# Two weight tiles of the first up chunk split into memory outside the ring

## The chip, the cores and the metric

The kernel runs on one core of a Trainium2 chip. The metric is the device time of one execution in microseconds (us). Times are the median of several executions; one further execution is recorded by the hardware profiler, and all rows quoted below are of that one.

## The reference

One decoder layer on 256 positions with width 2048, in float32:

```
h = rmsnorm(x);  p = h @ w_in                      # 2048 x 4160
A = 8 heads of dilated sliding-window attention from p
B = 8 heads of latent attention from p (w_uq, w_ukv)
x = x + rmsnorm(concat(A, B) @ w_out) * g1         # 2048 x 2048
h = rmsnorm(x)
x = x + rmsnorm(square(relu(h @ w_up)) @ w_down) * g2   # 2048 x 8192, 8192 x 2048
```

The change lies at the seam between `@ w_out` with its norm and the first columns of `@ w_up`.

## The kernel before, in words

**Products.** Each float32 matrix is split into a coarse part (`hi`) and a remainder (`lo`), and a product is three matmuls: hi·hi, lo·hi and hi·lo. One matmul takes 128 rows of the inner dimension and 512 columns. The 256 positions are two blocks, b = 0 and b = 1, of 128.

**Weights.** The class `Weights` holds a list of all weight tiles in the order of their use. Each tile is loaded by an SP DMA (SyncE's queue) into one of 5 `raw` buffers, and `split` or `split_gain` makes its two parts: ACT writes `hi` (L314, or L318 where a gain is multiplied in), DVE writes `lo` (L315 or L319). `hi` and `lo` come from a ring of 8 buffers each (`W_BUFS`), given out in turn. The order of the work on each engine is the order in which the program writes its instructions (the schedule is manual): what `emit` writes earlier stands earlier in ACT's, DVE's and SP's queues.

`get(i)` calls `emit(i + 1 + ahead)`, which writes the load and the split of every tile up to that index that isn't written yet, but at most 8 tiles beyond the first one that PE still needs (`limit`). `free(i)` tells that the last matmul of tile i has been written. `ahead` is 6; from the end of the out projection's block 0 until the end of the residual of block 1 it is 4 (`AHEAD_NORM`).

**The seam.** The out projection goes by chunks of 512 columns with 8 weight tiles each, of two 128-row blocks (I call the last chunk's tiles out 0 to out 7). In the last chunk out 0 to 2 are used for both blocks in turn, and then out 3 to 7 for block 0 and again for block 1, so that block 0's result is complete 5 tiles earlier (`APART[0]`). The up product's first chunk is 1024 columns in 16 tiles of 128 rows (up 0 to up 15), each worth 6 matmuls a block. Here up 0 to 6 are used for block 0, then up 0 to 6 for block 1, and then the rest for both in turn (`APART[1]` = 7). Thus up 0 to 6 stay in the ring until block 1's pass over them.

**The residual.** When block b of the last out chunk is complete, `out_evac` squares it on ACT (`junko`) and multiplies it by the gain on DVE (`yg`, L898). The generator `residual(b)` then makes the norm: DVE sums (`ssr`, L937) and scales (`t_post`, L505), POOL takes the power (`rstd_post`, L506), DVE updates the first two quarters of x (`x`, L943), and after that for each quarter n = 0 to 3: PE transposes it (`ht`, L308), DVE updates quarter n + 2 (n = 0 and 1 only), ACT writes `hT_hi` (L314), DVE writes `hT_lo` (L315). Quarter n holds the inner rows of up tiles 4n to 4n + 3. Behind the quarters follow four squares on ACT (`junkx`, L963), a sum (`ssr`, L965) and a scale (`t_pre`, L505) for the next norm. Residual 0 starts at the end of block 0's last matmul, residual 1 four planned microseconds after block 1's. `Flow` places these steps between matmuls by a clock that only matmuls and transposes advance (`pump` after every three matmuls); a weight split costs nothing on it.

The change uses two pieces of memory. `mixT` (a hi and a lo tile, 16 blocks of 256 columns) holds the heads' results, which the out projection reads; blocks 0 to 3 are read by out 0 and out 1. `po` is a pool of the out projection (gains, yg, x). Both pools are released just before up 8 is used, and a pool `up` takes their place.

Of the kernel before, what the change touches and what calls it, by code (L numbers as in the profile page):

```python
# [19 lines left out]
F32R = mybir.dt.float32r  # L20
# [6 lines left out]
P = 128  # L27
# [18 lines left out]
CW = 1024  # L46
# [30 lines left out]
APART = (5, 7)  # L77

FINE = 6

X_PIECES = ((2, 1, 1), (3, 2, 2), (5, 4, 3), (8, 7, 3), (11, 10, 3), (14, 13, 3))

# [53 lines left out]
class Flow:  # L136
# [3 lines left out]
    def __init__(self):  # L140
        self.clock = 0.0
        self.chains = []
# [34 lines left out]
class Weights:  # L177


    def __init__(self, nc, pool, split, bufs, ahead):  # L180
        self.nc, self.pool, self.split_fn = nc, pool, split
        self.bufs, self.limit, self.ahead = bufs, bufs, ahead
        self.specs, self.tiles, self.done = [], [], []
        self.first, self.after = {}, {}

    def plan(self, *spec):

# [11 lines left out]
        return raw  # L199

    def emit(self, upto):
        upto = min(upto, self.done.index(False) + self.limit, len(self.specs))
        while len(self.tiles) < upto:
            i = len(self.tiles)
            spec = self.specs[i]
            make = len(spec) == 1
            for f in self.first.pop(i, ()):
                f()
            if not make:
                src, nk, n, g = (*spec, None)[:4]  # L210
                w = nk * n
                raw = self.load(src if len(src.shape) == 3 else src.rearrange("(k p) n -> p k n", p=P), w, f"raw{i}")
                for f in self.after.pop(i, ()):
                    f()
            hi = self.pool.tile([P, CW], F32R, tag="hi", bufs=self.bufs, name=f"hi{i}")
            lo = self.pool.tile([P, CW], F32R, tag="lo", bufs=self.bufs, name=f"lo{i}")
            if make:
                spec[0](hi, lo)
                self.tiles.append((hi, lo))
                continue  # L220

            def v(t):
                return t[:, :w].rearrange("p (k n) -> p k n", k=nk)

            cuts = [(o, min(o + 512, w)) for o in range(0, w, 512)] if i < FINE else [(0, w)]
            for o, e in cuts:
                self.split_fn(hi[:, o:e], lo[:, o:e], raw[:, o:e], g)
            self.tiles.append((v(hi), v(lo)))
# [43 lines left out]
def layer(nc, tc, io):  # L272
    flow = Flow()

    def pool(name, side, **kw):
        return tc.alloc_tile_pool(name=name, bufs=1, side=side, **kw)
# [48 lines left out]
    weights = Weights(nc, wp, split, W_BUFS, W_AHEAD)  # L325
# [20 lines left out]
    def up_weight(j, k):  # L346
        return io["w_up"][k * P:(k + 1) * P, j * CW:(j + 1) * CW]

    late = {}
# [32 lines left out]
    def seven_up(j, kp):  # L382
        def load():
            if UP_PAIRS[j][kp] == "raw":
                return [weights.load(up_weight(j, 2 * kp + i), CW, f"raw_w{j}_{kp}{i}") for i in range(2)]
            return load_two(late[UP_PAIRS[j][kp]], nc.gpsimd if (j, kp) > (1, 0) else nc.sync,
                            io["w_up"][2 * kp * P:(2 * kp + 2) * P, j * CW:(j + 1) * CW])

        return seven(load, lambda: [late["up"].tile([P, CW], F32, tag="T", bufs=2, name=f"{n}{j}_{kp}") for n in "tu"])
# [21 lines left out]
    def plan_seven(fetch_sums, fs, after, more=(), late_sums=0, last=()):  # L411

        at = max(len(weights.specs) - SUMS_AHEAD, after)
        fetch, sums = fetch_sums
        for n, f in (*more, (0, fetch), (-late_sums, sums), *((0, f) for f in last)):
            weights.first.setdefault(at - n, []).append(f)
        return [weights.plan(f) for f in fs], len(weights.specs)
# [3 lines left out]
    wide_u, after = [], 0  # L421
    for j in range(FF // CW):
        wide_u.append([])
        for what, k in UP_STEPS[j]:
            if what == "k":

                ts = [weights.plan(up_weight(j, k), 1, CW, *([gcol[:, 8 + k:9 + k]] if j < 2 or k >= 2 * max(N_SEVEN) else []))]
            else:
                ts, after = plan_seven(*seven_up(j, k), after, (), SUMS_AHEAD + 1 if not k and N_SEVEN[j - 1] else 0)
            wide_u[j].append((what, k, ts))  # L430

    def down_weight(c, k):
        return io["w_down"][k * P:(k + 1) * P, c * CW:(c + 1) * CW]

    def seven_down(c, kp):
        def load():

            n = DOWN_SEVEN[c].index(kp)
            raw = dpl["ab"]
            if n % 2:  # L440
                raw = late["u01" if c else "c"]
            return load_two(raw, nc.gpsimd if c or n > 1 else nc.sync, io["w_down"][2 * kp * P:(2 * kp + 2) * P, c * CW:(c + 1) * CW])

        return seven(load, lambda: [late["st"][:, i * CW:(i + 1) * CW] for i in range(2)])

    dpl, left, skeep, wide_d = {}, {}, {}, []
    for c in range(2):
        wide_d.append([])
        for what, k in DOWN_STEPS[c]:
            if what == "k":  # L450
                ts = [weights.plan(down_weight(c, k), 1, CW)]
            else:
                q, parts_q, back = [lambda c=c, k=k, f=f: f(c, k) for f in (down_sums, down_split, down_back)]
                more = {"last": (back,)} if c and k in SHARED else {"more": ((2, q), (1, parts_q))}
                ts, after = plan_seven(*seven_down(c, k), after, **more)
# [8 lines left out]
    def proj(aT, chs, name, order=None, need=None, bank_of=None):  # L464
# [6 lines left out]
        for c, t, b in order:  # L471
# [4 lines left out]
            if need:  # L476
                need(k0 + kp - 1, b)
            if i[0] < FINE:
                hl = [(0, 0), (1, 0)], [(0, 1)]
# [33 lines left out]
    mixT = [mix.tile([P, HA + HB, S], F32R, name=f"mixT_{w}") for w in ("hi", "lo")]  # L513
# [201 lines left out]
    for half in range(2):  # L715
        qkv = {}
        for nms in (("qk", "v") if not half else "qkv"):
            accs = [acc for _, _, acc in proj(xT, [ch_a[half, nms]], f"{nms}{half}",
                                              bank_of=at_bank if (half, nms) == (0, "v") else None)]
            for i, nm in enumerate(nms):  # L720
                if half and nm == "v":
                    flow.finish(*heads)
                if not half and nm != "v":
                    t = early.tile([P, NB + 1, 512], F32, name=f"{nm}_{half}")
                else:
                    t = pa.tile([P, NB + (nm != "v"), 512], F32, tag=nm, name=f"{nm}_{half}")
# [134 lines left out]
    for what, ch in ch_b:  # L861
        if what == "qr":
            flow.finish(q_chain)
        if what in ("qr", "v0", "v1"):
            if what == "qr":
                qr = lat.tile([P, NB, HB, RB], F32, tag="cq", name="qr")
            for _, b, acc in proj(latT["q" if what == "qr" else "kv"], [ch], what):
                if what == "qr":
                    out = qr[:, b].rearrange("p h d -> p (h d)")
                else:  # L870
                    i = 4 * int(what[1])
# [4 lines left out]
        else:  # L876
            t, i = qT if what[0] == "q" else kT, 4 * int(what[1])
# [96 lines left out]
    def h_done(k, b):  # L974
        flow.until(lambda: 4 * parts[b] > k)

    res = [None] * NB
    for ns in ((0, 1), (2,), (3,)):
        if len(ns) == 2:
# [3 lines left out]
        for c, b, acc in proj(mixT, [ch_o[n] for n in ns], f"o{ns[0]}", order, heads_done):  # L983
            n = ns[c]
            if not late:
# [5 lines left out]
                po = late["po"] = pool("po", "right")  # L991
# [198 lines left out]
    for j in range(FF // CW):  # L1190
# [9 lines left out]
        for t, b in order:  # L1200
            what, k, tiles = steps[t]
# [189 lines left out]
    for g in (GT - 2, GT - 1):  # L1391
        for b, n in PARTS:
            for kk in range(4):
                k = 4 * g + kk
# [48 lines left out]
def build(nc, arrays):  # L1443
    io = {n: nc.dram_tensor(f"in_{n}", a.shape, mybir.dt.from_np(a.dtype), kind="ExternalInput").ap()
          for n, a in arrays.items()}
    io["out"] = nc.dram_tensor("out_0", (S, D), F32, kind="ExternalOutput").ap()
    with tile.TileContext(nc) as tc, tc.manual_schedule():
        layer(nc, tc, io)
# [12 lines left out]
```

## Time and profile before

| | |
|---|---|
| median of 3 runs | 1023.99 us (1022.15 to 1024.4) |
| profiled execution, its own time | 1021.68 us |
| its span | 1019.9 us |
| granted TensorE clock | 0.998 |
| PE (matmul) busy | 1009.6 us, 99% of the span |
| DVE busy | 839.7 us, 82% |
| ACT busy | 625.3 us, 61% |
| POOL busy | 98.3 us, 10% |
| DMA | 261 GB/s mean |

The rows of a timeline give start, duration, engine, line, operation, the tiles out<-in, shapes, the count, and in brackets how long the engine sat idle before it and what released it. A matmul's duration reaches over the next one's start, because matmuls are pipelined; the distance of starts tells how fast PE goes. Likewise on DVE and ACT one instruction's end overlaps the next one's start a little, so costs in a queue are taken as distances of starts.

### The profile page before, as it was taken

What the parts mean: (1) busy time and instruction counts of PE and PEld (TensorE: products, weight loads), DVE (VectorE), ACT (ScalarE), POOL (GpSimd) and SP (SyncE); (2) the same over time, 40 slices, a digit from 0 to 9 for tenths busy, and PEclk for the clock granted to TensorE, in tenths of its full rate; (3) what the DMA queues carried; (4) which work ended last, traced back from release to release, by engine and by line L of the source; (5) the groups of instructions that cost most, each with busy time, mean ns of one, the idle gap of its engine ahead of it and who ended that gap; (6) DMA issues with size and microseconds to landing.
All of it is one profiled execution on the core that took longest, in us unless ns stands there. A gap on an engine that the chain in (4) does not pass through costs nothing.

```text
span 1019.9 us, 13300 instructions
## 1 busy us (share of the span) xinstructions
PE 1009.6 (99%) x4678; PEld 842.4 (83%) x4678; DVE 839.7 (82%) x1125; ACT 625.3 (61%) x822; POOL 98.3 (10%) x156
## 2 busy tenths in 40 slices
PE   9999999999999999999999999999999999999996
PEld 6888889898888788888888888888888888888885
DVE  6676747676656779998999989898999989999885
ACT  6575436555454568576766776676666665767661
POOL 0020202002101200000010100000110000211100
PEclk9999999999999999999999999999999999999999
DMA  8977759555687477777988979679989867888952
GB/s 296 368 250 263 247 164 310 181 166 187 206 309 212 173 295 242 260 259 243 295 270 276 286 223 297 195 254 353 341 272 390 292 237 247 310 299 327 370 188 82
DMA packets 108850, 266.02 MB, mean 261 GB/s; under 512 B 9456, under 2 KB 28400, under 8 KB 108144
## 3 DMA queue, kind: packets, MB, share of 16 engines
q1 hardware_dynamic: 65584, 175.14, 50.1%
q0 software_dynamic: 19824, 70.27, 20.8%
q10 hardware_dynamic: 23376, 19.78, 6.2%
q8 instruction: 36, 0.59, 0.2%
q14 instruction: 30, 0.25, 0.1%
HBM read 232.12 MB, written 33.03 MB: 260 GB/s over the span
## 4 chain that ended last, share of the span: by engine, by line
PE 96%; DVE 1%; issue 1%; DMA 1%; ACT 0%; SPq 0%; POOL 0%; DVEq 0%; POOLq 0%; ACTq 0%
PE acc_u L304 26%; PE y L304 25%; PE acc_o L304 8%; PE md L304 6%; PE m L304 6%; PE acc_v L304 5%; PE acc_qk L304 4%; PE acc_q L304 3%; PE acc_k L304 3%; PE acc_ckv L304 3%; PE acc_cq L304 2%; PE sc_b L304 1%; PE acc_qr L304 1%; PE y L1329 1%; DMA raw<-in_w_in 1%
## 5 line engine op out<-in xcount | busy, mean ns | idle before, releaser
L315 DVE TENSOR_TENSOR lo<-raw,hi 128x1024 fp32r<-128x1024 f32 (+2 forms) x205 | 233.6, 1158 | 68.6 <-ACT hi L314 67.2
L314 ACT ACTIVATE hi<-raw 128x1024 fp32r<-128x1024 f32 (+2 forms) x205 | 202.8, 1004 | 76.1 <-DMA raw<-in_w_in 19.1
L304 PE MATMUL acc_u<-hi,hT_lo 128*128 128x512 f32 x386 | 150.3, 389 | 0.5 <-DVE hT_lo L315 0.5
L304 PE MATMUL acc_u<-hi,hT_hi 128*128 128x512 f32 x386 | 150.7, 390 | 0.0
L304 PE MATMUL acc_u<-lo,hT_hi 128*128 128x512 f32 x386 | 150.2, 389 | 0.0
L304 PE MATMUL y<-hi,uhi 128*128 128x512 f32 x358 | 139.3, 389 | 0.0
L304 PE MATMUL y<-lo,uhi 128*128 128x512 f32 x358 | 139.3, 389 | 0.0
L304 PE MATMUL y<-hi,ulo 128*128 128x512 f32 x358 | 139.3, 389 | 0.0
L318 ACT ACTIVATE hi<-raw,gcol 128x1024 fp32r<-128x1024 f32 x86 | 96.8, 1148 | 32.2 <-DMA raw<-in_w_up 12.0
L319 DVE SCALAR_TENSOR_TENSOR lo<-raw,gcol,hi 128x1024 fp32r<-128x1024 f32 x86 | 106.6, 1274 | 9.8 <-ACT hi L318 9.7
L304 PEld LDWEIGHTS acc_u<-hi,hT_lo 128*128 128x128 f32 x386 | 72.4, 188 | 15.9 <-DVE hT_lo L315 0.9
L304 PEld LDWEIGHTS acc_u<-hi,hT_hi 128*128 128x128 f32 x386 | 72.5, 188 | 14.9
L304 PEld LDWEIGHTS acc_u<-lo,hT_hi 128*128 128x128 f32 x386 | 72.5, 188 | 14.8
L304 PEld LDWEIGHTS y<-hi,ulo 128*128 128x128 f32 x358 | 67.2, 188 | 14.0
L304 PEld LDWEIGHTS y<-lo,uhi 128*128 128x128 f32 x358 | 67.2, 188 | 14.0
L304 PEld LDWEIGHTS y<-hi,uhi 128*128 128x128 f32 x358 | 67.2, 188 | 13.8
L315 DVE TENSOR_TENSOR lo<-st_down,hi 128x1024 fp32r<-128x1024 f32 x46 | 55.0, 1220 | 1.1 <-ACT hi L314 1.1
L304 PE MATMUL acc_o<-hi,mixT_hi 128*128 128x512 f32 x128 | 51.3, 401 | 0.0
L314 ACT ACTIVATE hi<-u 128x1024 fp32r<-128x1024 f32 (+1 forms) x33 | 32.3, 979 | 30.1 <-PE acc_u L304 12.3
L304 PE MATMUL md<-hi,s 128*128 128x512 f32 x138 | 50.0, 389 | 0.0
L304 PE MATMUL acc_o<-hi,mixT_lo 128*128 128x512 f32 x128 | 49.9, 390 | 0.0
L304 PE MATMUL acc_o<-lo,mixT_hi 128*128 128x512 f32 x128 | 49.8, 389 | 0.0
(353 smaller groups left out, 2042.3 us busy)
## 6 DMA issues: line engine op xcount, KB each, us to landing
raw<-in_w_up SPq DMA_DIRECT2D x86, 512.0 KB, 4.9
raw<-in_w_down SPq DMA_DIRECT2D x82, 512.0 KB, 6.1
raw<-in_w_in SPq DMA_DIRECT2D x55, 512.0 KB, 5.6
ab<-in_w_up POOLq DMA_DIRECT2D x17, 1024.0 KB, 7.2
raw<-in_w_out SPq DMA_DIRECT2D x32, 512.0 KB, 4.8
ab_down<-in_w_down POOLq DMA_DIRECT2D x11, 1024.0 KB, 9.3
ulo<-ukeep POOLq DMA_DIRECT2D x20, 512.0 KB, 6.0
rkeep<-r ACTq DMA_DIRECT2D x28, 256.0 KB, 3.7
```

The source lines that it names most:

```text
L304: nc.tensor.matmul(out, a, b, start=start, stop=stop)
L314: nc.scalar.activation(hi, src, AF.Copy)
L315: nc.vector.tensor_tensor(out=lo, in0=src, in1=hi.bitcast(F32), op=OP.subtract)
L318: nc.scalar.activation(hi, src, AF.Copy, scale=g)
L319: nc.vector.scalar_tensor_tensor(out=lo, in0=src, scalar=g, in1=hi.bitcast(F32), op0=OP.mult, op1=OP.subtract)
L1329: nc.tensor.matmul(out, a[x], w[z], start=False, stop=(x, z) == (1, 0), skip_group_check=True)
```

## The change

Tiles up 3 and up 4 no longer take buffers of the ring. `hi` and `lo` of up 3 are blocks 0 to 3 of the two `mixT` tiles; those of up 4 are two new tiles in the pool `po`. In `emit`, a lent tile doesn't count towards the limit of 8, and it is written whether the ring is full or not. Nothing is added to or taken from what is computed, loaded or split.

```
+LENT = 3, 4
...
     def emit(self, upto):
-        upto = min(upto, self.done.index(False) + self.limit, len(self.specs))
+        upto = min(upto, len(self.specs))
         while len(self.tiles) < upto:
             i = len(self.tiles)
+            own = [j for j in range(self.done.index(False), i) if j not in self.lent]
+            if i not in self.lent and len(own) >= self.limit:
+                return
             spec = self.specs[i]
...
-            hi = self.pool.tile([P, CW], F32R, tag="hi", bufs=self.bufs, name=f"hi{i}")
-            lo = self.pool.tile([P, CW], F32R, tag="lo", bufs=self.bufs, name=f"lo{i}")
+            if i in self.lent:
+                hi, lo = self.lent[i]()
+            else:
+                hi, lo = [self.pool.tile([P, CW], F32R, tag=t, bufs=self.bufs, name=f"{t}{i}") for t in ("hi", "lo")]
...
+    lent = [ts[0] for what, k, ts in wide_u[0] if k in LENT]
+    weights.lent = {lent[0]: lambda: [t[:, :4, :].rearrange("p k s -> p (k s)") for t in mixT],
+                    lent[1]: lambda: [late["po"].tile([P, CW], F32R, name=f"lent_{t}") for t in ("hi", "lo")]}
```

More of the change, by code (lines that the diff above doesn't have):

```diff
@@ L183, in __init__ @@
         self.specs, self.tiles, self.done = [], [], []
-        self.first, self.after = {}, {}
+        self.first, self.after, self.lent = {}, {}, {}
     def plan(self, *spec):
```

## The prediction

> **What bounds the kernel now.** I began with the shares of busy time and the waits of PE, then took the busy time by stretches, to see whether PE ever goes below its pace.
>
> ```profile
> PE 1009.6 (99%) x4678; PEld 842.4 (83%) x4678; DVE 839.7 (82%) x1125; ACT 625.3 (61%) x822; POOL 98.3 (10%) x156
> ...
> PE acc_qk L304 <- ACT hi L314: 0.5, 1, 0.5
> PE acc_u L304 <- DVE hT_lo L315: 0.5, 1, 0.5
> ...
> 357.60:675.00 317.40, 317.40 (x1401) 262.76 (x1401) 292.35 (x337) 217.18 (x255) 20.17 (x26) 1.00 0.81 261
> 675.00:1006.00 331.00, 331.00 (x1462) 274.08 (x1461) 302.64 (x348) 207.58 (x236) 32.24 (x52) 1.00 0.81 290
> ```
>
> PE is the bound. In the last two rows it starts 1401 and 1462 matmuls in 317.40 and 331.00 us, 0.2266 and 0.2264 us each: one constant pace with the clock at 1.00, so there is nothing to gain behind 357.6 us, and a shift of PE there goes through to the end. Of the waits recorded for PE, that of acc_u for hT_lo lies at the seam that the change touches. So I read PE's own order of time there.
>
> ```profile
> 342.23 0.60 PE L308 MATMUL ht<-ident,x 128*128 128x128 f32 x4
> 344.06 0.60 PE L308 MATMUL ht<-ident,x 128*128 128x128 f32 x4
> ...
> 350.44 0.39 PE L304 MATMUL acc_u<-hi,hT_lo 128*128 128x512 f32 x1
> 350.73 0.63 PE L308 MATMUL ht<-ident,x 128*128 128x128 f32 x4
> 351.12 0.48 PE L304 MATMUL acc_u<-hi,hT_hi 128*128 128x512 f32 x1
> ...
> 353.25 0.40 PE L304 MATMUL acc_u<-lo,hT_hi 128*128 128x512 f32 x1
> 354.12 0.50 PE L304 MATMUL acc_u<-hi,hT_lo 128*128 128x512 f32 x1 [0.47 <-DVE hT_lo L315]
> ```
>
> The first two are block 0's transposes of quarters 2 and 3, the one at 350.73 is block 1's of quarter 0. The matmul at 354.12 is the first that needs block 1's hT_lo. By the pace it would have started at 353.25 + 0.23 = 353.48, so PE loses 0.64 us. Another 0.06 us goes at 350.73 (due at 350.44 + 0.23 = 350.67). **All that stands to be gained at the seam is 0.70 us of some 1022.** What could be lost has no such cap: whatever moves that hT_lo later, moves the end. What stands ahead of it is in DVE's queue:
>
> ```profile
> 328.39 1.28 DVE L319 SCALAR_TENSOR_TENSOR lo<-raw,gcol,hi 128x1024 fp32r<-128x1024 f32 x1 [1.43 <-ACT hi L318]
> 334.79 0.69 DVE L898 TENSOR_TENSOR yg<-acc_o,g_post 128x512 f32<-128x512 f32 x1 [5.11 <-ACT junko L897]
> ...
> 340.88 1.28 DVE L319 SCALAR_TENSOR_TENSOR lo<-raw,gcol,hi 128x1024 fp32r<-128x1024 f32 x1 [0.35 <-ACT hi L318]
> ...
> 343.94 1.28 DVE L319 SCALAR_TENSOR_TENSOR lo<-raw,gcol,hi 128x1024 fp32r<-128x1024 f32 x1
> 345.14 0.68 DVE L315 TENSOR_TENSOR hT_lo<-ht,hT_hi 128x512 fp32r<-128x512 f32 x1
> 345.74 1.27 DVE L319 SCALAR_TENSOR_TENSOR lo<-raw,gcol,hi 128x1024 fp32r<-128x1024 f32 x1
> 346.93 0.68 DVE L315 TENSOR_TENSOR hT_lo<-ht,hT_hi 128x512 fp32r<-128x512 f32 x1
> 347.53 1.28 DVE L319 SCALAR_TENSOR_TENSOR lo<-raw,gcol,hi 128x1024 fp32r<-128x1024 f32 x1
> 348.73 0.15 DVE L937 TENSOR_REDUCE ssr<-ssy 128x1 f32<-128x4 f32 x1
> 348.91 0.27 DVE L505 TENSOR_SCALAR t_post<-ssr,pws 128x1 f32<-128x1 f32 x1
> 349.88 1.41 DVE L943 SCALAR_TENSOR_TENSOR x<-yg,rstd_post,x 128x512 f32<-128x512 f32 x2 [0.70 <-POOL rstd_post L506]
> 351.21 1.28 DVE L319 SCALAR_TENSOR_TENSOR lo<-raw,gcol,hi 128x1024 fp32r<-128x1024 f32 x1
> 352.41 0.15 DVE L965 TENSOR_REDUCE ssr<-ssx 128x1 f32<-128x4 f32 x1
> 352.59 0.21 DVE L505 TENSOR_SCALAR t_pre<-ssr,pws 128x1 f32<-128x1 f32 x1
> 352.72 0.74 DVE L943 SCALAR_TENSOR_TENSOR x<-yg,rstd_post,x 128x512 f32<-128x512 f32 x1
> 353.38 0.68 DVE L315 TENSOR_TENSOR hT_lo<-ht,hT_hi 128x512 fp32r<-128x512 f32 x1
> ```
>
> From 343.94 to 354.06 (353.38 + 0.68) DVE has one pause, 0.70 us for POOL's power. The splits (L319) in it are, by the order of emission: up 2 at 328.39, up 3 at 340.88, up 4 at 343.94, up 5 at 345.74, up 6 at 347.53, up 7 at 351.21. Distances of starts give the prices in this queue: a split 1.20 (347.53 to 348.73), an hT_lo 0.60, an update of x 0.66 (352.72 to 353.38). ACT stands beside it:
>
> ```profile
> 327.21 1.15 ACT L318 ACTIVATE hi<-raw,gcol 128x1024 fp32r<-128x1024 f32 x1 [1.57 <-PE acc_o L304]
> 334.07 0.60 ACT L897 ACTIVATE junko<-acc_o 128x512 bf16<-128x512 f32 x1 [5.71 <-PE acc_o L304]
> ...
> 342.39 1.14 ACT L318 ACTIVATE hi<-raw,gcol 128x1024 fp32r<-128x1024 f32 x1
> 343.43 0.59 ACT L314 ACTIVATE hT_hi<-ht 128x512 fp32r<-128x512 f32 x1
> 343.91 1.15 ACT L318 ACTIVATE hi<-raw,gcol 128x1024 fp32r<-128x1024 f32 x1
> 344.95 0.59 ACT L314 ACTIVATE hT_hi<-ht 128x512 fp32r<-128x512 f32 x1
> 345.42 1.15 ACT L318 ACTIVATE hi<-raw,gcol 128x1024 fp32r<-128x1024 f32 x1
> 347.85 1.14 ACT L318 ACTIVATE hi<-raw,gcol 128x1024 fp32r<-128x1024 f32 x1
> ...
> 350.17 0.18 ACT L963 ACTIVATION_READ_ACCUMULATOR junkx<-x 128x1 f32 x1
> 351.40 0.60 ACT L314 ACTIVATE hT_hi<-ht 128x512 fp32r<-128x512 f32 x1 [1.04 <-PE ht L308]
> ```
>
> **What the change moves.** First, up 3 and up 4. In block 0's pass over out 3 to 7 the ring is full with out 3 to 7 and up 0 to 2; with `ahead` 6, `get` asks for up 3 at out 5 and up 4 at out 6, and the limit refuses them. Lent tiles aren't refused, so both splits now stand behind up 2's and ahead of block 0's junko and yg. There ACT is idle for 5.71 us and DVE for 5.11 us (the brackets at 334.07 and 334.79). Two hi of 1.15 and two lo of 1.28 fit: from 327.21 + 1.15 = 328.36 on ACT, and on DVE done at about 332.3, before 334.79. Their data are there, by the SP queue:
>
> ```profile
> 322.03 1.47 SPq L198 DMA_DIRECT2D raw<-in_w_up  x2
> ...
> raw<-in_w_up SPq DMA_DIRECT2D x5, 512.0 KB, 3.6
> ```
>
> The two loads are up 3's and up 4's, and land 3.6 us after issue (the median of the stretch). Shapes and engines of the splits stay the same, so I price them the same in lent memory. **Cost of this step: nothing, hidden in those two pauses.**
>
> Second, up 8 and up 9, which the change's words don't mention. In block 0's pass over the up tiles `ahead` is 4, so `get` asks for up 8 at up 4 and for up 9 at up 5. Before, the limit of 8 refused both, as up 0 to 7 held the ring, and they were split in block 1's pass, behind all that is shown above. Now up 3 and up 4 don't count, so 6 tiles are in the ring at up 4 and 7 at up 5: both are accepted. Block 1's quarter 0 (transposes, update of quarter 2, hT_hi, hT_lo) is written after up 5's last matmul. **So two splits leave DVE's queue ahead of that hT_lo, and two others enter it, later, between the update of quarters 0 and 1 and the hT_lo.** On ACT, two hi enter ahead of block 1's first hT_hi.
>
> What is won ahead of `ssr` (348.73)? The lo of up 3 and up 4 are gone, 2 × 1.20 = 2.40 us of DVE, but then another thing ends last. Block 0's hT_hi of quarter 2 can start once its transposes end, 342.23 + 0.60, say 342.87; up 5's hi 0.48 later (343.43 to 343.91), at 343.35, and ends at 344.50. DVE's lo of up 5 goes from there, the hT_lo of quarter 3 1.20 later at 345.73, and the lo of up 6 at 346.33. ACT gives the same limit: quarter 3's transposes end at 344.66, hT_hi at 344.70, up 6's hi 0.47 later (344.95 to 345.42) and 1.15 long, done at 346.32. So `ssr` comes at 346.33 + 1.20 = 347.53, **1.20 us earlier**, and the other 1.20 is lost waiting for PE's transposes, whose place in PE's order is fixed. Bounds: 0 (something in the crowd keeps it) and 2.40.
>
> What is added behind it? From `ssr` at 347.53: x at 348.68 (1.15 later, as from 348.73 to 349.88), the lo of up 7 at 350.01 (1.33), the sum at 351.21, the lo of up 8 at 351.52 (0.31), of up 9 at 352.72, x of quarter 2 at 353.92, hT_lo at 354.58, done at 355.26, PE at 355.32 with the 0.06 that it took before (354.06 to 354.12). ACT isn't later: shifted by 0.25 like up 6's hi, its last junkx ends at 350.10, two hi at 1.04 each (343.91 to 344.95) bring hT_hi to 352.18 and its end to 352.78, while DVE gets there only at 354.58. **Sum: −1.20 + 2.40 = +1.20 us**, PE's wait being 355.32 − 353.42 = 1.90 us in place of 0.64 + 0.06.
>
> The rest costs nothing. The SP loads of up 8 and up 9 go out when up 3's and up 4's raw buffers come free, in about 331 to 332.3 us; only further weight loads stand behind them, each waiting for a raw buffer anyway, and by 3.6 us they land before ACT wants them at 350. POOL's queue gets and loses nothing. The buffers of the ring that the later tiles take are those of out 3 to 7, free by the end of the out projection. In block 1's pass DVE has 2.40 us less to do, but PE waits for nothing there. The pool `up` now also waits for block 1's reads of up 3 and up 4, which end before up 8 starts; its first user comes after 8 steps of 12 matmuls, 8 × 12 × 0.2266 = 21.8 us.
>
> [...] The trace shows a single gap, not a repeating one, and its releaser is hT_lo, not a weight, so by the rows the extra room lets more weight work in ahead of what PE waits for.
>
> **Rivals.**
> [...]
> 2. *Nothing is won ahead of ssr*, because ACT or DVE finds another wait between 339 and 347: then the two added splits count in full, +2.40 us. For it: DVE and ACT are both nearly full there. Against it: the rows worked out above.
> 3. *The lent memory brings a wait of its own, slower.* If the write into `mixT` were ordered against reads of the whole tile, out 5's matmuls for block 0 would stand behind up 3's split: hi 1.15, lo 1.28, with hand-overs some 2.6 us of PE, and with the +1.20 that makes +3.8. It decides as soon as any PE read is tied to the whole tile. Against it: at 351.12 PE reads block 0 of hT_hi while block 1's write to the same tile, which stands ahead of it in the program, starts only at 351.40. So dependences go by region.
>
> **How the numbers follow.** The profiled execution took 1021.68 us, 2.31 below the median of the runs shown, 1023.99; the term is a shift of PE and is added to either: 1022.88 for a profiled execution of the same kind, 1025.2 for the median. Rival 1 gives 1023.3, rival 2 1026.4, rival 3 1027.8. Chances: the forecast 0.70, rival 1 0.14, rival 2 0.10, rival 3 0.06. The range reaches from below rival 1 to above rival 2, with some 0.5 us at each end for the spread of the runs shown (1022.15 to 1024.4): 1022.8 to 1026.9. A measurement of this kernel can tell about 0.2%, 2.05 us, from no change. Slower by more are rival 3, two thirds of rival 2, and the forecast in about one case of ten: 0.06 + 0.07 + 0.07 = 0.20. No case gains that much; spread alone leaves 0.03. The same: 0.77.
>
> **What would show it.** Right: two lo (L319) directly behind the one at 328.39; `ssr` near 347.5; three lo, not one, between the x at about 348.7 and block 1's first hT_lo; PE's wait for hT_lo about 1.3 us longer than its 0.47; the SP loads of up 8 and up 9 near 331. [...] A PE wait for a weight's lo behind 357 us would be something that I have not seen.

## The result, and the profile after

| | runs | median | ratio to before (95%) |
|---|---|---|---|
| before, beside the change | 12 | 1022.42 us | |
| the change | 12 | 1025.03 us | 1.0024 [1.0016, 1.0032] |
| the change once more, in a later session (before: 27 runs, 1022.44 us) | 11 | 1023.77 us | 1.0014 [1.0005, 1.0023] |

The change made the kernel slower, by 2.5 us in the first comparison (1.6 to 3.3) and by 1.4 us in the second (0.5 to 2.4). The profiled execution took 1025.6 us with a span of 1023.8 us, 3.9 us longer than the span of before.

PE's waits in the changed kernel:

```profile
PE acc_u L311 <- DVE hT_lo L322: 1.8, 1, 1.8
PE warm L534 <- DVE zero L531: 1.2, 1, 1.2
PE acc_qk L311 <- ACT hi L321: 0.6, 3, 0.3
```

The wait for hT_lo at the seam was 0.5 us and is 1.8 us. The DVE queue that leads to it (start, duration, line, operation):

```profile
328.64 1.28 DVE L326 SCALAR_TENSOR_TENSOR lo<-raw,gcol,hi 128x1024 fp32r<-128x1024 f32 x1 [1.44 <-ACT hi L325]
329.85 1.28 DVE L326 SCALAR_TENSOR_TENSOR mixT_lo<-raw,gcol,mixT_hi 128x1024 fp32r<-128x1024 f32 x1
331.04 1.28 DVE L326 SCALAR_TENSOR_TENSOR lent_lo<-raw,gcol,lent_hi 128x1024 fp32r<-128x1024 f32 x1
335.04 0.69 DVE L905 TENSOR_TENSOR yg<-acc_o,g_post 128x512 f32<-128x512 f32 x1 [2.71 <-ACT junko L904]
...
346.62 1.28 DVE L326 SCALAR_TENSOR_TENSOR lo<-raw,gcol,hi 128x1024 fp32r<-128x1024 f32 x1
347.82 0.15 DVE L944 TENSOR_REDUCE ssr<-ssy 128x1 f32<-128x4 f32 x1
348.01 0.27 DVE L512 TENSOR_SCALAR t_post<-ssr,pws 128x1 f32<-128x1 f32 x1
348.98 1.41 DVE L950 SCALAR_TENSOR_TENSOR x<-yg,rstd_post,x 128x512 f32<-128x512 f32 x2 [0.70 <-POOL rstd_post L513]
350.31 2.47 DVE L326 SCALAR_TENSOR_TENSOR lo<-raw,gcol,hi 128x1024 fp32r<-128x1024 f32 x2
352.70 0.15 DVE L972 TENSOR_REDUCE ssr<-ssx 128x1 f32<-128x4 f32 x1
352.88 0.21 DVE L512 TENSOR_SCALAR t_pre<-ssr,pws 128x1 f32<-128x1 f32 x1
353.01 1.27 DVE L326 SCALAR_TENSOR_TENSOR lo<-raw,gcol,hi 128x1024 fp32r<-128x1024 f32 x1
354.21 0.74 DVE L950 SCALAR_TENSOR_TENSOR x<-yg,rstd_post,x 128x512 f32<-128x512 f32 x1
354.87 0.68 DVE L322 TENSOR_TENSOR hT_lo<-ht,hT_hi 128x512 fp32r<-128x512 f32 x1
```

The names in the second and third row say where up 3 and up 4 went, into the pause ahead of yg, of which 2.71 us is left. Between x at 348.98 and block 1's first hT_lo at 354.87 stand three splits in place of one: up 7, up 8 and up 9. What PE does there:

```profile
353.42 0.40 PE L311 MATMUL acc_u<-lo,hT_hi 128*128 128x512 f32 x1
355.61 0.69 PE L311 MATMUL acc_u<-hi,hT_lo 128*128 128x512 f32 x1 [1.79 <-DVE hT_lo L322]
356.09 0.63 PE L311 MATMUL acc_u<-hi,hT_hi 128*128 128x512 f32 x1
356.52 0.63 PE L311 MATMUL acc_u<-lo,hT_hi 128*128 128x512 f32 x1
356.94 0.63 PE L311 MATMUL acc_u<-hi,hT_lo 128*128 128x512 f32 x1
357.37 1.05 PE L315 MATMUL ht<-ident,x 128*128 128x128 f32 x4
...
359.59 0.40 PE L311 MATMUL acc_u<-lo,hT_hi 128*128 128x512 f32 x1
359.82 0.40 PE L311 MATMUL acc_u<-hi,hT_lo 128*128 128x512 f32 x1
```

PE loses 355.61 − 353.42 − 0.23 = 1.96 us. Then comes what no row of before had: the next matmuls start 0.43 us apart, not 0.23. Busy time by stretches shows why; the number before the last two is the granted clock.

```profile
352.30:355.60 3.30, 1.52 (x9) 0.95 (x7) 3.27 (x7) 1.23 (x3) 1.51 (x1) 1.00 0.86 254
355.60:359.10 3.50, 3.49 (x11) 2.82 (x12) 1.22 (x3) 0.60 (x1) 2.13 (x4) 0.52 0.92 352
359.10:362.60 3.50, 3.50 (x19) 2.90 (x18) 1.37 (x2) 1.88 (x5) 0.00 (x0) 0.99 0.39 157
```

In the 3.5 us behind the gap the clock is 0.52 on average. PE looks busy all the while (3.49 of 3.50), but starts 11 matmuls where it starts 19 in the next stretch of that length.

I matched the starts of the same matmuls in the two traces. The profiled execution of the change is 0.26 us later already at the start of the kernel. It falls back by a further 1.23 us up to the matmul behind the gap (offset 1.49), by 1.59 us in the half-clock stretch (offset 3.08 at 359.36), and by some 0.9 us in two places far behind, near 656 and 752 us on the scale of before.

### The profile page after: what moved, and what is told of

It is laid out like the page before. It is cut to its first block, busy times and chain, and to the rows that moved or that the text cites. A ratio compares the mean times of both kernels' runs of the same rounds, so it can differ in the third digit from the quotient of the medians.

```text
span 1023.8 us, 13296 instructions
## 1 busy us (share of the span) xinstructions
PE 1011.8 (99%) x4678; PEld 843.3 (82%) x4678; DVE 839.8 (82%) x1125; ACT 624.5 (61%) x822; POOL 99.1 (10%) x156
## 4 chain that ended last, share of the span: by engine, by line
PE 80%; DVE 9%; DMA 3%; issue 3%; ACT 3%; ACTq 1%; POOL 0%; DVEq 0%; POOLq 0%; SPq 0%
PE y L311 19%; PE acc_u L311 19%; PE acc_o L311 9%; PE acc_v L311 5%; PE md L311 5%; PE m L311 4%; PE acc_qk L311 4%; DVE lo L322 3%; PE acc_q L311 3%; PE acc_k L311 3%; PE acc_ckv L311 2%; DVE lo L326 2%; PE acc_cq L311 2%; DMA rkeep<-uT 1%; PE sc_b L311 1%
## 5 line engine op out<-in xcount | busy, mean ns | idle before, releaser
L311 PE MATMUL acc_u<-hi,hT_lo 128*128 128x512 f32 x378 | 147.7, 391 | 1.8 <-DVE hT_lo L322 1.8
L311 PE MATMUL acc_u<-hi,hT_hi 128*128 128x512 f32 x378 | 148.1, 392 | 0.0
L311 PE MATMUL acc_u<-lo,hT_hi 128*128 128x512 f32 x378 | 147.7, 391 | 0.1
L325 ACT ACTIVATE hi<-raw,gcol 128x1024 fp32r<-128x1024 f32 x84 | 94.5, 1148 | 34.0 <-DMA raw<-in_w_up 14.7
L326 DVE SCALAR_TENSOR_TENSOR lo<-raw,gcol,hi 128x1024 fp32r<-128x1024 f32 x84 | 103.9, 1273 | 5.7 <-ACT hi L325 5.7
```

What stands on the lines that cost most here:

```text
L311: nc.tensor.matmul(out, a, b, start=start, stop=stop)
L325: nc.scalar.activation(hi, src, AF.Copy, scale=g)
L326: nc.vector.scalar_tensor_tensor(out=lo, in0=src, scalar=g, in1=hi.bitcast(F32), op0=OP.mult, op1=OP.subtract)
```

## The experiments

Theory: the pair up 8 and up 9, let in ahead of block 1's first hT_lo, makes PE's gap, and the gap can halve the clock behind it. Rival A: lending the memory, or splitting up 3 and up 4 early, costs by itself. Rival B: the fall of the clock has nothing to do with the gap.

**The lent pair early, all later tiles where they were.** Lent tiles count towards the limit of the others:

```
-            own = [j for j in range(self.done.index(False), i) if j not in self.lent]
+            own = range(self.done.index(False), i)
```

> Up 3 and up 4 are lent and split early as in the change, but they count towards the limit of every later tile, so up 8 and up 9 are split where they were before. Theory (the added pair up 8 and up 9 in DVE's queue makes the loss): PE's wait for hT_lo is gone, the clock stays at 1.00 through the seam, and the time is 0.7 us below before (-0.07%). Rival A (the lent memory or the early place of up 3 and up 4 costs by itself): it stays some 2.5 us above before. Rival B (the half clock behind the seam is chance and has nothing to do with the wait): clock may fall here too.

Measured: 1022.06 us, ratio 0.9996 [0.9986, 1.0006]. Its rows of DVE, without those between:

```profile
347.32 0.15 DVE L944 TENSOR_REDUCE ssr<-ssy 128x1 f32<-128x4 f32 x1
349.80 1.28 DVE L326 SCALAR_TENSOR_TENSOR lo<-raw,gcol,hi 128x1024 fp32r<-128x1024 f32 x1
351.97 0.69 DVE L322 TENSOR_TENSOR hT_lo<-ht,hT_hi 128x512 fp32r<-128x512 f32 x1
```

its PE at the place of the gap:

```profile
352.91 0.40 PE L311 MATMUL acc_u<-lo,hT_hi 128*128 128x512 f32 x1
353.15 0.40 PE L311 MATMUL acc_u<-hi,hT_lo 128*128 128x512 f32 x1
```

and its busy time and clock behind it:

```profile
352.50:356.00 3.50, 3.50 (x22) 2.89 (x19) 2.17 (x4) 1.20 (x2) 2.13 (x4) 1.00 0.69 273
```

One split is left between, hT_lo ends at 352.66 before PE wants it, and the two matmuls stand 0.24 us apart: the gap is closed. By the matched starts the seam gives back 0.82 us, 0.09 of it at the transposes at 350.73 and the rest at hT_lo. The time can't be told from that of before, since the interval is ±1.0 us. It lies clear of the change's first comparison (from 1.0016), and its interval touches that of the second (from 1.0005). Rival A is refuted: the trace shows no cost of the lent memory or of the early place, and the time leaves room for less than 1 us.

**The other half alone.** `LENT = 8, 9`, and the pools released at up 10 rather than up 8:

```
-LENT = 3, 4
+LENT = 8, 9
...
-            if (j, t, b) == (0, 8, 0):
+            if (j, t, b) == (0, 10, 0):
```

> The same memory is lent to up 8 and up 9 instead, and the two pools are released two tiles later, so up 3 and up 4 stay in their old places and up 8 and up 9 come early: the other half of the change alone. Theory: ssr stays near 348.7 us on before's scale, three lo stand between x and block 1's first hT_lo, PE loses 0.64 + 2.40 = 3.0 us at that matmul, then runs at half clock for some 3.5 us (another 1.5 us): +2.4 + 1.5 = +3.9 us against before. Rival A: about 0, since up 3 and up 4 aren't moved. Rival B: +2.4 us, with the clock at 1.00.

Measured: 1026.78 us, ratio 1.0039 [1.0025, 1.0052], that is +4.0 us. PE at the gap:

```profile
354.03 0.40 PE L311 MATMUL acc_u<-lo,hT_hi 128*128 128x512 f32 x1
356.73 0.50 PE L311 MATMUL acc_u<-hi,hT_lo 128*128 128x512 f32 x1 [2.29 <-DVE hT_lo L322]
```

and the busy time and clock behind it:

```profile
356.70:357.70 1.00, 0.97 (x4) 0.81 (x5) 1.00 (x2) 0.00 (x0) 0.08 (x1) 1.00 0.98 360
357.70:361.30 3.60, 3.60 (x13) 2.85 (x12) 0.92 (x2) 0.60 (x1) 2.05 (x4) 0.54 0.88 356
```

A gap of 2.47 us, preceded by a wait of some 0.5 us for hT_hi, together the 3.0 us expected. Here ACT too is late: PE sat idle for 0.28 us ahead of its matmul at 353.70, which waited for ACT's hT_hi. About 1.2 us after PE went on, the clock falls: its mean is 1.00 from 356.70 to 357.70 and 0.54 in the 3.60 us behind that. By the matched starts the gap costs 2.4 us and the clock 1.6 us; the expectation counted the fall in every execution, where the mean clock below shows it in 5 of 10. So the early pair alone makes the whole loss; the early split of up 3 and up 4 softened it.

**Only up 3 lent.** One tile leaves, one comes:

```
-LENT = 3, 4
+LENT = 3,
...
-    weights.lent = {lent[0]: lambda: [t[:, :4, :].rearrange("p k s -> p (k s)") for t in mixT],
-                    lent[1]: lambda: [late["po"].tile([P, CW], F32R, name=f"lent_{t}") for t in ("hi", "lo")]}
+    weights.lent = {lent[0]: lambda: [t[:, :4, :].rearrange("p k s -> p (k s)") for t in mixT]}
```

> Only up 3 is lent: one split leaves the crowd, and only up 8 comes early. Theory: ssr some 0.4 us earlier, one added lo of 1.2 us, so PE's lost time at hT_lo goes from 0.64 to about 1.4 us, +0.8 us against before; if a gap of 1.4 us is enough to halve the clock, +2.3 us. Rival A: between 0 and +2.5, half of the change's loss, some +1.2 us. Rival B: the clock's fall doesn't depend on this gap.

Measured: 1023.31 us, ratio 1.0007 [0.9999, 1.0016]. The matmuls at 354.17 and 355.94 leave a gap of 1.54 us, and the clock stays at 1.00 behind it (the stretch 355.9 to 359.4 us). The theory's first number was +0.8 us; the matched starts give +0.84 us at the seam and the times +0.7 us. The time by itself is unclear, since its interval reaches from −0.1 to +1.6 us.

**The change with PE kept at work.** Eight matmuls that nobody reads, ahead of block 1's first matmuls:

```
+                if (j, t, b) == (0, 0, 1):
+                    fill = at_bank("fill")
+                    for _ in range(N_FILL):
+                        nc.tensor.matmul(fill, tok(hT[0], 0, 0), w[0][:, 0, :512], start=True, stop=True)
```

> The change with 8 added matmuls (1.8 us, into a bank that nobody reads, on operands that are long there) ahead of block 1's first matmuls, so that PE works while it would wait for hT_lo; they change nothing in the output. Theory (the gap makes the clock fall): the wait for hT_lo shrinks to some 0.1 us, the following matmuls stay 0.227 us apart, and the time is +1.2 us against before, some 1.5 us less than the change's own profiled execution. Rival B (clock unrelated to the gap): the half clock stays for some 3.5 us behind it, and the time is that of the change, +2.5 us.

Measured: 1024.02 us, ratio 1.0012 [1.0003, 1.0021], +1.2 us. The added matmuls in PE's rows:

```profile
354.13 2.10 PE L1234 MATMUL fill<-hi,hT_hi 128*128 128x512 f32 x8
```

and the busy time and clock with them and behind:

```profile
354.10:356.70 2.60, 2.60 (x14) 1.86 (x12) 2.60 (x5) 0.60 (x1) 1.51 (x1) 1.00 0.88 290
356.70:360.20 3.50, 3.50 (x20) 2.92 (x21) 1.85 (x3) 0.65 (x2) 2.13 (x4) 1.00 0.96 369
```

DVE is as late as in the change, but PE isn't idle, and the clock stays at 1.00. What is left, +1.26 us at the seam by the matched starts, is the price of DVE's lateness alone. It is what I had predicted for the change. The time alone doesn't tell this run from the second comparison of the change (1.0014); the clock does, below for all executions.

**The change once more.**

> The change once more, unaltered. Theory (the pair up 8 and up 9 in DVE's queue, and a gap on PE that can halve the clock behind it): the lost time at block 1's first hT_lo is again some 1.9 us; where the clock then falls the span is some 2.8 us above before, where it doesn't some 1.2 us, so the runs' spans lie in two groups about 1.5 us apart; the median is 1.5 to 2.8 us above before. Rival B (the clock's fall is unrelated): one group, or falls at other places too.

Measured: the ratio 1.0014 of the table above. The profiled execution had the same gap (352.42 to 354.62, 1.97 us), but its busy time and clock by stretches read:

```profile
352.30:354.60 2.30, 0.52 (x3) 0.07 (x1) 2.30 (x4) 0.60 (x1) 1.40 (x1) 1.00 0.91 333
354.60:358.10 3.50, 3.48 (x19) 2.96 (x20) 1.92 (x3) 0.60 (x1) 2.14 (x4) 1.00 0.90 348
```

Here the clock did not fall: 19 matmuls in 3.5 us, and a span of 1021.7 us. So with a gap of this length it falls in some executions only. Whether the spans lie in two groups, as expected, can't be told: those of before alone spread over 3 us (27 executions, 1019.5 to 1022.6 us), twice the distance that was looked for. The mean granted clock of each execution tells more. A stretch of 3.41 us at half clock takes 3.41 × 0.5 / 1023.8 = 0.0017 off it, and in the profiled executions the mean was 0.995 or 0.996 with a fall and 0.997 or 0.998 without one. It is 0.996 or less in 7 of the first 12 executions of the change, but in 2 of these 11. By an estimate from these shares, (7/12 − 2/11) × 1.59 = 0.6 us of the 1.1 us between the two comparisons comes from the clock; the rest lies within their intervals.

**DVE work in place of the early pair.** The version with all later tiles in place, and in `residual(1)`, ahead of the first hT_lo, two instructions of a split's size whose results nobody reads:

```
+            if (n, b) == (0, 1):
+                for w_ in EXTRA:        # CW, CW
+                    nc.vector.scalar_tensor_tensor(out=yg[0][:, :w_], in0=xs[0][:, :w_], scalar=r, in1=xs[0][:, :w_],
+                                                   op0=OP.mult, op1=OP.subtract)
```

> The version where up 3 and up 4 are lent and all later tiles keep their places, with two added DVE instructions of a split's size (128x1024, results that nobody reads) ahead of block 1's first hT_lo. No weight is split earlier than in that version. Theory (it is only DVE's time in that place that counts): lost time at hT_lo 1.9 us as in the change, +1.2 us against before with the clock at 1.00 and +2.7 us where it halves, like the change. Rival A (the early pair costs by its memory, its loads or ACT's part): clearly less than the change, since ACT and the loads aren't touched.

Measured: 1024.56 us, ratio 1.0022 [1.0013, 1.0032], the change's loss without the early pair. The added work in DVE's rows:

```profile
351.15 2.60 DVE L963 SCALAR_TENSOR_TENSOR yg<-x,rstd_post 128x1024 f32<-128x1024 f32 x2
353.67 0.75 DVE L951 SCALAR_TENSOR_TENSOR x<-yg,rstd_post,x 128x512 f32<-128x512 f32 x1
354.33 0.68 DVE L323 TENSOR_TENSOR hT_lo<-ht,hT_hi 128x512 fp32r<-128x512 f32 x1
```

PE at the gap:

```profile
352.75 0.40 PE L312 MATMUL acc_u<-lo,hT_hi 128*128 128x512 f32 x1
355.07 0.62 PE L312 MATMUL acc_u<-hi,hT_lo 128*128 128x512 f32 x1 [1.92 <-DVE hT_lo L323]
```

and the clock behind it:

```profile
355.00:358.50 3.50, 3.43 (x11) 2.75 (x12) 1.28 (x4) 0.60 (x1) 2.14 (x4) 0.54 0.38 150
```

So it is DVE's time in that place, not memory, loads or ACT: the same gap and the same fall come without them.

**Half as much in the second instruction** (`EXTRA = CW, 512`), **and three of them** (`EXTRA = CW, CW, CW`).

> As with the two added DVE instructions, but the second is half as wide (1.20 + 0.60 us). Lost time at hT_lo some 1.3 us. Theory: +0.6 us against before; the clock stays at 1.00, as it did after a gap of 1.5 us in the run with one lent tile. If any gap of PE halves the clock, +2.1 us.

> As with the two added DVE instructions, but three of them (3.6 us). Lost time at hT_lo some 3.1 us. Theory: the clock halves for some 3.5 us behind the gap in every execution, +2.4 + 1.5 = +3.9 us against before and one group of spans. If the clock's fall is unrelated to the gap's length, +2.4 us in about half of the runs.

Measured: 1022.82 us, 1.0004 [0.9995, 1.0013], for the first; 1028.09 us, 1.0053 [1.0038, 1.0069], from four runs, for the second. The first has a gap of 1.56 us (352.95 to 354.74; 0.2 longer than I had worked out), and the busy time and clock behind it are:

```profile
354.70:358.20 3.50, 3.46 (x19) 2.93 (x20) 1.94 (x3) 0.60 (x1) 2.14 (x4) 1.00 0.38 150
```

The clock stays at 1.00. The second has a gap of 3.41 us (355.01 to 358.65), and behind it:

```profile
358.60:359.60 1.00, 0.95 (x4) 0.81 (x5) 1.00 (x2) 0.00 (x0) 0.06 (x1) 1.00 0.00 0
359.60:363.10 3.50, 3.50 (x13) 2.73 (x11) 0.95 (x2) 0.60 (x1) 2.08 (x4) 0.51 0.66 265
```

The second cost +5.4 us (3.9 to 7.1) where I expected +3.9; its seam gives 2.7 for the gap and 1.6 for the clock by the matched starts. The mean clock is 0.996 or less in all four of its executions.

Together: the gap at hT_lo in the profiled execution, the clock in the 3.5 us behind it (or behind 1.0 us more), and in how many executions the mean granted clock is 0.996 or less (of before, those beside the experiments).

| kernel | gap, us | clock behind | executions at 0.996 or less | ratio |
|---|---|---|---|---|
| lent pair early, rest in place | 0 | 1.00 | 0 of 12 | 0.9996 |
| before | 0.64 | 1.00 | 1 of 60 | 1 |
| only up 3 lent | 1.54 | 1.00 | 0 of 12 | 1.0007 |
| 1.5 DVE instructions | 1.56 | 1.00 | 0 of 10 | 1.0004 |
| the change | 1.96 | 0.52 | 7 of 12 | 1.0024 |
| the change once more | 1.97 | 1.00 | 2 of 11 | 1.0014 |
| 2 DVE instructions | 2.09 | 0.54 | 4 of 11 | 1.0022 |
| up 8 and 9 lent | 2.47 | 0.54 | 5 of 10 | 1.0039 |
| 3 DVE instructions | 3.41 | 0.51 | 4 of 4 | 1.0053 |

Rival B is refuted. The mean clock is low in 22 of 48 executions with a gap of 1.96 us or more. It is low in none of 46 of the versions with a shorter gap or with the gap filled (0 of 12 there).

How long the low stretch lasts is in the traces as well. These rows of the change are the last tenths of a microsecond ahead of each step of the clock, and the first behind it:

```profile
355.66:355.76 0.10, 0.10 (x1) 0.10 (x2) 0.10 (x1) 0.00 (x0) 0.00 (x0) 0.98 0.84 287
355.77:355.87 0.10, 0.10 (x1) 0.10 (x2) 0.10 (x1) 0.00 (x0) 0.00 (x0) 0.50 1.16 328
359.07:359.17 0.10, 0.10 (x2) 0.09 (x1) 0.08 (x1) 0.00 (x0) 0.00 (x0) 0.50 2.25 902
359.18:359.28 0.10, 0.10 (x2) 0.10 (x1) 0.10 (x1) 0.00 (x0) 0.00 (x0) 1.00 0.82 328
```

The clock is at 0.50 from 355.76 to 359.17, for 3.41 us. For the other three profiles with a fall I estimate the length from the mean clocks of the stretches, taking the low clock as 0.50: with two DVE instructions 0.54 in the 3.50 us from 355.00 and 0.97 in the next 3.50, (0.46 + 0.03) × 3.50 / 0.5 = 3.4 us; with up 8 and 9 lent 0.54 in the 3.60 us from 357.70 and 0.99 in the next 2.70, (0.46 × 3.60 + 0.01 × 2.70) / 0.5 = 3.4 us; with three DVE instructions 0.51 in the 3.50 us from 359.60 and 1.00 behind, 0.49 × 3.50 / 0.5 = 3.4 us.

In these nine profiles the clock fell behind four of the five gaps of 1.96 us or more, and behind none of the three of 0.64 to 1.56 us. What decides near 2 us was not shown: a gap of 1.96 us had the fall and one of 1.97 us, in the same program, had not. Nor does one length of idle time precede each fall: the clock also falls behind the end of PE's work, in the change at 1017.94, 2.2 us after the last matmul's end (1015.32 + 0.39), and in before at 1015.47, 3.7 us after it (1011.38 + 0.39).

## Why the prediction was right, and what it missed

The predicted 1025.2 us met 1025.03. That is partly luck: it stood on a median of before of 1023.99 us, where more runs gave 1022.42. The step predicted, +1.2 us, lies below the first comparison's interval (+1.6 to +3.3) and inside the second's (+0.5 to +2.4). For a profiled execution the prediction had 1022.88 us; the first one took 1025.6 us and the later one, without the fall of the clock, 1023.45 us.

- *What moves.* Right in each row named: two lo behind the one at 328.64, three between x and hT_lo, and the loads of up 7 to up 9 from 329.96 us, as SP's queue has it:

```profile
329.96 2.72 SPq L200 DMA_DIRECT2D raw<-in_w_up  x3
```

- *What is won ahead of ssr.* Predicted 347.53, measured 347.82 with PE 0.26 later from the start on, so 347.56. The limit by PE's transposes, which halved the gain, held.
- *What is lost behind it.* PE's gap was to be 1.90 us and was 1.96; filled with work, it cost +1.26 against the predicted +1.20. The cap of 0.70 us on the gain was a little low: the version that closes the gap gave back 0.82 us, because the matmul behind the wait in before is also followed 0.33 us later (354.12 to 354.45) and not 0.23.
- *The step that failed:* "a shift of PE there goes through to the end", taken as the whole price of a gap. The shift does go through, but a gap of about 2 us may also halve the clock for 3.41 us, 1.59 us more in the profiled execution. The trace of before had no gap longer than 0.64 us behind its start, and I priced a gap at its own length without asking whether a longer one is still of the same kind.
- *The rivals.* The gap's closing (rival 1, 1023.3 us) needed up 8 and up 9 to stay back: with that one line changed it closes (hT_lo's end at 352.66 in that run, PE's matmul at 353.15, 0.24 us behind the one before it). The third, a wait by the lent memory, did not occur: PE's only wait on the first chunk is that for hT_lo. More room made the single gap longer, from 0.64 to 1.96 us, because the room went to work that wasn't urgent.
- *Not foreseen and not settled:* the 0.9 us near 656 and 752 us. PE loses some 0.3 us at a time on a matmul that reads a weight's lo (from 659.04 to 659.54 us in the change, 0.27 above the pace), in stretches where DVE never pauses (there from 654.52 to 663.47 us). The prediction had named such a wait as something not seen before. Several of the profiled executions show such waits, in differing size, also without a fall of the clock (two of 0.3 us in the change once more, one of 0.2 us with PE kept at work); the one of before shows none. I did not find what sets them.

## What to carry to other kernels

More buffers for a look-ahead don't only free the tiles that they were meant for: ask which further work the look-ahead now lets in, and whether it lands in an engine's queue ahead of something that the bound engine waits for, as two lo did on DVE here (PE's gap went from 0.64 to 1.96 us). Here the memory was harmless and the limit, one line, was the loss. And where PE is the bound, price an idle gap by its own length only as long as gaps of that length leave the clock unchanged, in more than one execution: here the same gap of 2 us halved it in one profile and not in another.

## What the runs showed of the hardware

In the change the granted clock fell to 0.50 behind an idle gap of 1.96 us. It stayed there for 3.41 us, and then was at 1.00 again (from 359.18 us) though PE worked at the low clock (busy for 3.49 of 3.50 us). It fell as well behind gaps of 2.09, 2.47 and 3.41 us, where its mean in the stretch behind was 0.54, 0.54 and 0.51, for about 3.4 us each by the estimate above. The fall started 0.15 us (the change) after PE went on, and by the same means about 0.2 us (two DVE instructions), 1.0 us (three of them) or 1.2 us (up 8 and 9 lent) after it. A gap of 1.97 us left the clock at 1.00 in another execution of the same program. Gaps of 1.54 and 1.56 us left it at 1.00 in the one profile that each has, and none of these 22 executions has a low mean clock.
